# Ordering one more burst of state-space products, and moving the delta rule's output norm to GpSimd

## The chip, the cores and the metric

The kernel runs on one core of one Trainium2 chip. The metric is the device time of one execution in microseconds (us); less is better. TensorE does matmuls and transposes (PE in the profile, with its weight loads as PEld), VectorE is DVE, ScalarE is ACT, GpSimd is POOL, and SyncE (SP) issues the DMAs.

## The reference, cut to what matters

Two layers of a decoder trunk, 512 tokens, 1024 channels, float32. Each layer norms x, projects it into three branches (a chunked state-space scan, latent attention, a gated delta rule), merges them with sigmoid gates, and adds a squared-ReLU feed-forward. The change touches two branches. In the state-space scan, for each chunk of 128 tokens (a "block" below), the part within the block is

```python
L = jnp.exp(jnp.where(tril, A_cum[..., :, None] - A_cum[..., None, :], -jnp.inf))
CB = jnp.einsum('bclgn,bcsgn->bcgls', Cc, Bc)
y_diag = jnp.einsum('bcgls,bgecls,bcsgep->bclgep', CB, L, X)
```

and in the delta rule the recurrence's output o is normed per head and gated:

```python
o = gated_delta_chunked(q, k, v, g, beta)
o = rmsnorm(o, norm_g) * jax.nn.silu(z.astype(jnp.float32).reshape(Bsz, S, GDN_V_HEADS, GDN_HEAD_V))
```

## The kernel before, in words

Everything is float32. The large products (projections, output products, feed-forward) are made as three passes of a split operand: a weight tile of 128x512 is cast on ScalarE to its high part (`whi`, L170), VectorE subtracts to get the low part (`wlo`, L171), and TensorE adds high times high, high times low and low times high (`mm3`, L198 to L200). There are four buffers of each part. These products make up most of the program; below they are called the dense products. Their outputs sit in four PSUM banks (`acc`). Small products (state-space, delta rule, transposes) run in plain float32, into three further banks (`sm`, `sm_bank()`) and one called `yt`.

A framework orders the instructions of each engine when the program is built: by priority, which is mostly the order of the program text, among those that its own model of time finds ready. On the chip each engine then runs its list strictly in order. The small products come earlier in the text than the dense products of the stage after them, so the framework fits them among these. `place(key, ins)` notes a dense product under (tag, row k, column j), and `behind(key, ins)` forces a small product to stand after the noted one on TensorE's list; this is an order at build time and no wait on the chip.

`ssd_group(g, ...)` handles one half of the state-space branch (g is 0 or 1), for the four blocks t = 0 to 3. For each block it makes the decay tiles `e2` (two of four heads each; four buffers `eE`), multiplies them by the masked product `cb` of L782, and then makes the eight decay products of L791, each with 64 output columns, two heads side by side into halves of one bank, `py`. L802 is the carried state's part (`po`), L809 the new state (`pst`), L823 a sum of squares. The dense products that surround it are those of `out_proj` for the attention branch, tags (ly, 1, 2g, "g") and (ly, 1, 2g, "y"). The L791 products of blocks 0 and 3 are put behind named rows; those of blocks 1 and 2 are left to the framework.

`gdn_unit(u, ...)` handles four of the delta rule's eight heads, again over four blocks t. Its chain from block to block is: L1067 (state times keys), L1070 (DVE), L1073 (`pw`), L1078 and L1084 (`vn` on DVE, `vd` on ACT), L1087 (`pS`), L1096 (new state, DVE). Off that chain it makes the output: L1099 (`po`), L1106 (`pq`), ACT copies `po` to the tile `o` (L1107, or L1111 in block 0), DVE adds `pq` (L1109), ACT takes the squares' sums into `ss` (L1115). Then DVE makes the norm's factor `ms` from `ss` and the query's norm (L1119 to L1124, with a power -0.5 on GpSimd at L277), and scales: `gz = gz * ms * o`, one instruction per head (L1127). The tile `o` has one buffer (`wk3`), so L1107 of a block waits until L1127 of the block before has read it. After the four blocks, L1132 transposes `gz`. Around unit 0 run the dense products of unit 1's keys and values with their convolutions (L724 on ACT, L728 three times on DVE for each bank), around unit 1 those of `out_proj` for the delta branch.

Of the kernel before, what the change touches and what calls it, by code (L numbers as in the profile page):

```python
# [10 lines left out]
F32 = mybir.dt.float32  # L11
# [4 lines left out]
ALU = mybir.AluOpType  # L16
# [4 lines left out]
P = 128  # L21
S = 512
T = S // P
D = 1024
KD = D // P
EPS = 1e-6
# [29 lines left out]
def hybrid_kernel(ctx, tc, a, out, depth=2, taps=None):  # L56
    nc = tc.nc
    pe, act, dve, pool, sync = nc.tensor, nc.scalar, nc.vector, nc.gpsimd, nc.sync
    uid = itertools.count()

    def mk(pl, shape, dt, tag, bufs=None):
        return pl.tile(shape, dt, tag=tag, name=f"{tag}_{next(uid)}", bufs=bufs)
# [12 lines left out]
    def bc_last(ap, n):  # L75
        sh = list(ap.shape)
        return ap.unsqueeze(len(sh)).to_broadcast(sh + [n])

    cst = ctx.enter_context(tc.tile_pool(name="cst", bufs=1))
    sp = ctx.enter_context(tc.tile_pool(name="sp", bufs=1))  # L80
# [9 lines left out]
    def y_bank():  # L90
        return mk(ps_sm, [P, 512], F32, "yt", 1)

    def sm_bank():
        return mk(ps_sm, [P, 512], F32, "sm")
# [11 lines left out]
    nhalf = mk(cst, [P, 32], F32, "nhalf")  # L106
# [43 lines left out]
    def after_product(i, o):  # L150
        tc.add_manual_dep(i, o.name, order_only, reason="behind a product")

    def behind(key, ins):

        if key in seen_at:
            after_product(ins.ins, seen_at[key])
        else:
            awaiting.setdefault(key, []).append(ins.ins)
# [116 lines left out]
    def rsq(o, ss, scale, eps, exp=None):  # L275
        dve.tensor_scalar(o, ss, scale, eps, ALU.mult, ALU.add)
        pool.tensor_tensor(o, o, (exp if exp is not None else nhalf)[:, : o.shape[1]], ALU.pow)  # L277
# [106 lines left out]
    for ly in range(depth):  # L384
# [97 lines left out]
        def seg_exp(o, t, h0):  # L482

            of = o.rearrange("p i l -> p (i l)")
            sync.dma_start(of, d_c[t, h0 * P : (h0 + 4) * P].partition_broadcast(P))
            for i in range(4):
                act.activation(o[:, i], o[:, i], AF.Relu, scale=-1.0, bias=cum[:, t, h0 + i : h0 + i + 1])  # L487
            act.activation(of, of, AF.Exp, scale=-1.0)
# [99 lines left out]
        for hp in range(4):  # L588
# [68 lines left out]
            for j in range(2):  # L657
# [3 lines left out]
                for t in range(T):  # L661
                    n = max(256, (t + 1) * P)
                    tok = slice(t * P, (t + 1) * P)
                    ps = sm_bank()
                    o = ps[:, :n]
# [5 lines left out]
                    n = (t + 1) * P  # L671
                    o = ps[:, :n]
# [9 lines left out]
                for kbs in ((0,), (1,), (3, 2)):  # L682
                    ps = sm_bank()
                    n = 0
# [14 lines left out]
                    for kb, c0, c in parts:  # L699
                        v_h, v_l = (x[:, kb, :] for x in vs[j])  # L700
                        o = po[:, c0:]
# [34 lines left out]
        br = bp.enter_context(tc.tile_pool(name="br", bufs=1, reuse_waits="tile"))  # L736


        def ssd_group(g, yh, yl):
# [12 lines left out]
            for t in range(T):  # L752
                x = pe.transpose(ps[:, t * P : (t + 1) * P], bt[:, t * P : (t + 1) * P], ident)
# [19 lines left out]
            c4 = lambda x: x.rearrange("p (c l) -> p c l", c=4)  # L773
            pss = y_bank()
            st = None
            for t in range(T):
                tok = slice(t * P, (t + 1) * P)
                e2 = [mk(br, [P, 4, P], F32, "eE", 4) for _ in range(2)]
                for q in range(2):
                    seg_exp(e2[q], t, h0 + 4 * q)  # L780
                ps = sm_bank()
                pe.matmul(ps[:, :P], bt[:, tok], ctl[:, tok], start=True, stop=True)  # L782
                cb = mk(br, [P, P], F32, "gk", 2)
                dve.scalar_tensor_tensor(cb, ps[:, :P], 0.25, incl, ALU.mult, ALU.mult)
                for e in e2:
                    dve.tensor_tensor(e, e, bc_mid(cb, 4), ALU.mult)
                py = sm_bank()
                for c in range(4):
                    for i in range(2):
                        h = 2 * c + i  # L790
                        x = pe.matmul(py[64 * i : 64 * i + 64, c * P : (c + 1) * P], xd[:, t, h * 64 : (h + 1) * 64], e2[h // 4][:, h % 4, :], start=True, stop=True)  # L791
                        if t in (0, T - 1):
                            behind(((ly, 1, 2 * g, "g"), 2, 0) if t == 0 else ((ly, 1, 2 * g, "y"), 3, 0), x)
                y = xf[:, :, tok]
                dve.tensor_tensor(y, y, c4(py), ALU.add)
                if t > 0:
                    eb = mk(br, [P, 4, P], F32, f"wk{t % 2}")
                    for i in range(2):
                        sync.dma_start(eb[64 * i : 64 * i + 64], d_p.rearrange("t (n l) -> t n l", l=P)[t, h0 + i : h0 + 8 : 2].partition_broadcast(64))
                    po = sm_bank()  # L800
                    for c in range(4):
                        pe.matmul(po[:, c * P : (c + 1) * P], st[:, c * P : (c + 1) * P], ctl[:, tok], start=True, stop=True)  # L802
                    dve.tensor_tensor(eb, c4(po), eb, ALU.mult)
                    dve.tensor_tensor(y, y, eb, ALU.add)
                if t < T - 1:
                    xe = mk(br, [P, 512], F32, "wk3")
                    dve.tensor_tensor(hv8(xe), hv8(xd[:, t, :]), bc_last(dec[:, 1, t, h0 : h0 + 8], 64), ALU.mult)
                    pst = sm_bank()
                    pe.matmul(pst, btok[:, t, :], xe, start=True, stop=True)  # L809
                    sn = mk(br, [P, 512], F32, "st", 2)  # L810
                    if t == 0:
                        act.copy(sn, pst)
                    else:
                        dve.tensor_tensor(hv8(sn), hv8(st), bc_last(dec[:, 2, t, h0 : h0 + 8], 64), ALU.mult)
                        dve.tensor_tensor(sn, sn, pst, ALU.add)
                    st = sn
                zt = z[:, :, tok]
                dve.tensor_tensor(zt, zt, y, ALU.mult)
                sq = mk(br, [P, 4, P], F32, "wk2")
                act.activation(sq, zt, AF.Square)  # L820
                dve.tensor_tensor(sq[:, 0:2], sq[:, 0:2], sq[:, 2:4], ALU.add)
                dve.tensor_tensor(sq[:, 0], sq[:, 0], sq[:, 1], ALU.add)
                x = pe.matmul(pss[:, t : t + 1], sq[:, 0], ones[:, 0:1], start=True, stop=True)  # L823
                if t > 1:
                    behind(((ly, 1, 2 * g, "y"), 4 * t - 5, 0), x)
# [19 lines left out]
        hv = lambda x: x.rearrange("p (h n) -> p h n", h=4)  # L845
# [159 lines left out]
        def gdn_unit(u, kT, ork, cc, cd, Yt, yh, yl):  # L1005
# [10 lines left out]
            rq = mk(sp, [P, 2, T], F32, "grq", 2)  # L1016
# [8 lines left out]
            gz = mk(br, [P, T, 512], F32, "tok", 5)  # L1025
            for i in range(2):
                for j, pj in enumerate(dense_F(weights(w_in, O_GV + (4 * u + 2 * i) * P, 256, D), tiles(256), D, xh, xl, tag=(ly, "v", 4 * u + 2 * i))):
                    h = 2 * i + j
# [3 lines left out]
                    for t in range(T):  # L1032
                        x = pe.transpose(ps[:, t * P : (t + 1) * P], vf[:, t * P : (t + 1) * P], ident)
# [5 lines left out]

            hdec = lambda i, t, h: dec[:, i, t, hd0 + h : hd0 + h + 1]  # L1040
            ss = mk(sp, [P, T, 4], F32, "gos", 2)
            g_, y_ = ((ly, 2, i // 2, "gy"[i % 2]) for i in range(2))
            seq = [(ly, "k", 2), (ly, "v", 4), (ly, "v", 6)] if u == 0 else [g_, y_, (ly, 2, 1, "g")]
            pw_place = (seq[0], 3, 0), (seq[0], 7, 0), (seq[1], 2, 0)
# [4 lines left out]
            for t in range(T):  # L1049
# [5 lines left out]
                for i in range(2):  # L1055
                    x = pe.matmul(pg[:, i * P : (i + 1) * P], kT[i][:, tok], qT[i][:, tok], start=True, stop=True)
# [15 lines left out]
                for h in range(4):  # L1072
                    x = pe.matmul(pw[:, h * P : (h + 1) * P], Y[:, h, :], r[:, h * P : (h + 1) * P], start=True, stop=True)  # L1073
# [6 lines left out]
                if t < T - 1:  # L1080
# [5 lines left out]
                    for i in range(2):  # L1086
                        x = pe.matmul(pS[:, i * 256 : (i + 1) * 256], ktok[i][:, t, :], vd[:, i * 256 : (i + 1) * 256], start=True, stop=True)  # L1087
# [10 lines left out]
                for h in range(4):  # L1098
                    x = pe.matmul(po[:, h * P : (h + 1) * P], pt_[:, h, :], vn[:, h * P : (h + 1) * P], start=True, stop=True)  # L1099
                    if t == T - 1:  # L1100
                        behind((seq[1], 2, 1), x)
                o = mk(br, [P, 512], F32, "wk3")
                if t > 0:
                    pq = sm_bank()
                    for i in range(2):
# [8 lines left out]
                    jk = mk(br, [P, P], F32, "gk", 2)  # L1114
                    act.activation(jk, o[:, h * P : (h + 1) * P], AF.Square, accum_out=ss[:, t, h : h + 1])  # L1115

                rqt = mk(sp, [P, 4], F32, "grt", 2)
                for j in range(2):
                    dve.tensor_scalar(rqt.rearrange("p (i j) -> p i j", j=2)[:, :, j], rq[:, :, t], 128.0 ** -0.5, None, ALU.mult)  # L1119
                ms = mk(sp, [P, 4], F32, "gms", 2)  # L1120
                dve.tensor_tensor(ms, ss[:, t, :], rqt, ALU.mult)
                dve.tensor_tensor(ms, ms, rqt, ALU.mult)
                rsq(ms, ms, 1.0 / 128, EPS)
                dve.scalar_tensor_tensor(ms, ms, 0.5, rqt, ALU.mult, ALU.mult)  # L1124
                for h in range(4):
                    gzh = hv(gz[:, t, :])[:, h]
                    dve.scalar_tensor_tensor(gzh, gzh, ms[:, h : h + 1], hv(o)[:, h], ALU.mult, ALU.mult)  # L1127
            for c in range(4):
                k = 4 * u + c
                ps = y_bank()  # L1130
                for t in range(T):
                    x = pe.transpose(ps[:, t * P : (t + 1) * P], gz[:, t, c * P : (c + 1) * P], ident)  # L1132
# [132 lines left out]
        with tc.tile_pool(name="wo", bufs=1, reuse_waits="tile") as wo:  # L1265
# [8 lines left out]
            h = mk(hpl, [P, T, D], F32, "h")  # L1274
# [209 lines left out]
```

## Time and profile before

| what | value |
|---|---|
| median of 3 runs | 2274.53 us (2274.5 to 2274.64) |
| the profiled execution | 2274.29 us, of which the profile's span is 2272.5 us |
| PE busy | 2252.4 us, 99% of the span |
| DVE busy | 1649.5 us, 73% |
| ACT busy | 1186.1 us, 52% |
| POOL busy | 65.0 us, 3%, 84 instructions |
| granted TensorE clock | 0.999 |

A profile row of the timeline gives start, duration, engine, line, operation, the tiles written and read, and how many instructions were merged. A plain float32 matmul leaves two records. In a row of the waits, the numbers are total us, how often, and the longest. The shown end of a matmul is modelled, and matmuls overlap; the distance from start to start tells what one cost.

### The profile page before, as it was taken

The numbers are of one execution on the slowest core, as the hardware profiler recorded it, in microseconds if no ns is written. First come the engines' busy times: TensorE is split into PE (matmuls) and PEld (weight loads), VectorE is DVE, ScalarE is ACT, GpSimd is POOL, SyncE is SP. The second block draws the span as 40 slices with busy tenths as digits, with TensorE's granted clock in tenths as the row PEclk, the third lists the DMA queues.
The fourth block names the chain that finished last, engine by engine and source line by source line (L and its number), as shares of the span: only waits on it lengthen the run. The fifth ranks groups of instructions, "written<-read, shape, count | busy, mean of one in ns | idle before, by whom it ended". The sixth has DMA issues, their size and how long they took to land.

```text
span 2272.5 us, 32127 instructions
## 1 busy us (share of the span) xinstructions
PE 2252.4 (99%) x11758; PEld 1867.6 (82%) x11758; DVE 1649.5 (73%) x3315; ACT 1186.1 (52%) x2444; POOL 65.0 (3%) x84
## 2 busy tenths in 40 slices
PE   9999999999999999999999999999999999999998
PEld 8888888888888888888888878888888887888886
DVE  7886567776766778767868865678657667778668
ACT  6666744333443555554656667443344435645545
POOL 1000000000000000000010000000001000000000
PEclk9999999999999999999999999999999999999999
DMA  4223633442225143233132246335422251433231
GB/s 143 81 75 110 190 108 119 137 134 75 84 65 176 56 149 111 93 110 103 52 99 81 71 121 195 104 110 148 121 84 75 66 189 34 167 112 102 84 111 47
DMA packets 220030, 244.07 MB, mean 107 GB/s; under 512 B 34256, under 2 KB 172384, under 8 KB 219872
## 3 DMA queue, kind: packets, MB, share of 16 engines
q1 hardware_dynamic: 219872, 242.02, 34.7%
q8 instruction: 92, 1.51, 0.3%
q14 instruction: 66, 0.54, 0.1%
HBM read 225.53 MB, written 11.74 MB: 104 GB/s over the span
## 4 chain that ended last, share of the span: by engine, by line
PE 95%; DVE 3%; DMA 1%; ACT 1%; issue 0%; POOL 0%; SPq 0%; DVEq 0%; POOLq 0%; ACTq 0%
PE acc L198 24%; PE acc L200 24%; PE acc L199 24%; PE sm L200 3%; PE sm L199 3%; PE sm L198 3%; PE sm L687 1%; PE sm L791 1%; DVE wlo L171 1%; PE yt L703 1%; PE sm L1073 1%; PE sm L802 1%; PE sm L1099 1%; PE yt L200 1%; PE yt L199 1%; PE yt L198 1%
## 5 line engine op out<-in xcount | busy, mean ns | idle before, releaser
L171 DVE TENSOR_TENSOR wlo<-wraw,whi 128x512 fp32r<-128x512 f32 (+1 forms) x536 | 365.4, 686 | 336.3 <-ACT whi L170 325.3
L170 ACT CAST whi<-wraw 128x512 fp32r<-128x512 f32 (+1 forms) x536 | 329.5, 618 | 524.1 <-PE acc L199 339.7
L198 PE MATMUL acc<-xh,whi 128*128 128x512 f32 (+1 forms) x1344 | 525.3, 391 | 0.0
L200 PE MATMUL acc<-xh,wlo 128*128 128x512 f32 (+1 forms) x1344 | 520.4, 388 | 0.0
L199 PE MATMUL acc<-xl,whi 128*128 128x512 f32 (+1 forms) x1344 | 519.2, 387 | 0.0
L200 PEld LDWEIGHTS acc<-xh,wlo 128*128 128x128 f32 x1344 | 252.5, 188 | 49.3
L198 PEld LDWEIGHTS acc<-xh,whi 128*128 128x128 f32 x1344 | 252.5, 188 | 48.4 <-ACT xh L272 0.4
L199 PEld LDWEIGHTS acc<-xl,whi 128*128 128x128 f32 x1344 | 252.7, 188 | 47.6 <-DVE xl L273 0.7
L170 ACT CAST whi<-wr 128x512 fp32r<-128x512 f32 x168 | 104.3, 621 | 107.9 <-PE acc L199 47.7
L198 PE MATMUL acc<-yh,whi 128*128 128x512 f32 x384 | 152.1, 400 | 0.0
L199 PE MATMUL acc<-yl,whi 128*128 128x512 f32 x384 | 150.3, 391 | 0.0
L200 PE MATMUL acc<-yh,wlo 128*128 128x512 f32 x384 | 149.8, 390 | 0.0
L171 DVE TENSOR_TENSOR wlo<-wr,whi 128x512 fp32r<-128x512 f32 x168 | 113.1, 685 | 35.6 <-ACT whi L170 34.7
L728 DVE SCALAR_TENSOR_TENSOR ckl<-acc,pc,ckl 128x511 f32<-128x511 f32 (+2 forms) x168 | 121.2, 743 | 19.2 <-ACT ckl L724 10.9
L198 PEld LDWEIGHTS acc<-yh,whi 128*128 128x128 f32 x384 | 71.5, 188 | 16.4 <-ACT yh L272 2.2
L200 PEld LDWEIGHTS acc<-yh,wlo 128*128 128x128 f32 x384 | 72.1, 188 | 15.1
L199 PEld LDWEIGHTS acc<-yl,whi 128*128 128x128 f32 x384 | 72.1, 188 | 14.2
L198 PE MATMUL acc<-whi,xh 128*128 128x512 f32 (+1 forms) x208 | 80.3, 386 | 1.2 <-DVE ckl L728 1.2
L199 PE MATMUL acc<-wlo,xh 128*128 128x512 f32 (+1 forms) x208 | 79.3, 381 | 0.0
L200 PE MATMUL acc<-whi,xl 128*128 128x512 f32 (+1 forms) x208 | 79.2, 382 | 0.0
L1219 DVE TENSOR_TENSOR h<-h,acc 128x512 f32<-128x512 f32 x120 | 76.9, 679 | 1.3 <-PE acc L200 1.3
L487 ACT ACTIVATE eE<-eE,cum 128x128 f32<-128x128 f32 x192 | 62.5, 390 | 27.9 <-DMA eE<-d_c 26.2
(468 smaller groups left out, 4497.8 us busy)
## 6 DMA issues: line engine op xcount, KB each, us to landing
wraw<-in_w_in_dram SPq DMA_DIRECT2D x144, 512.0 KB, 3.6
wraw<-in_w_up_dram SPq DMA_DIRECT2D x64, 512.0 KB, 3.5
wr<-in_w_down_dram SPq DMA_DIRECT2D x32, 1024.0 KB, 5.1
eE<-d_c SPq DMA_DIRECT2D x48, 256.0 KB, 4.1
wraw<-in_w_mla_out_dram SPq DMA_DIRECT2D x16, 512.0 KB, 3.4
eE<-d_e SPq DMA_DIRECT2D x32, 256.0 KB, 2.9
wraw<-in_w_ssd_out_dram SPq DMA_DIRECT2D x16, 512.0 KB, 3.3
wraw<-in_w_gdn_out_dram SPq DMA_DIRECT2D x16, 512.0 KB, 3.5
```

The source lines that it names most:

```text
L170: act.copy(hi, raw)
L171: dve.tensor_tensor(lo, raw, f32(hi), ALU.subtract)
L198: pe.matmul(o, ah, bh, start=start, stop=False, skip_group_check=more)
L199: pe.matmul(o, ah, bl, start=False, stop=False, skip_group_check=more)
L200: return pe.matmul(o, al, bh, start=False, stop=stop, skip_group_check=more)
L487: act.activation(o[:, i], o[:, i], AF.Relu, scale=-1.0, bias=cum[:, t, h0 + i : h0 + i + 1])
L687: pe.transpose(ps[:, n : n + P], pn[t][:, kb * P : (kb + 1) * P], ident)
L703: pe.matmul(o, v_h, th[:, c : c + w], start=kb == 0, stop=False)
L728: dve.scalar_tensor_tensor(acc[:, d:], ps[:, : S - d], taps_[3 - d], acc[:, d:], ALU.mult, ALU.add)
L791: x = pe.matmul(py[64 * i : 64 * i + 64, c * P : (c + 1) * P], xd[:, t, h * 64 : (h + 1) * 64], e2[h // 4][:, h % 4, :], start=True, stop= ...
L802: pe.matmul(po[:, c * P : (c + 1) * P], st[:, c * P : (c + 1) * P], ctl[:, tok], start=True, stop=True)
L1219: dve.tensor_tensor(hs_, hs_, ps[t], op)
```

## The change

Three edits, all in the two functions above.

1. The L791 products of block 1 are put behind row 4, column 1 of (ly, 1, 2g, "g"). Blocks 0 and 3 keep their places.
2. The tile `o` of the delta rule alternates between the buffers `wk3` and `wk0` from block to block.
3. The norm's factor and the scaling go from VectorE to GpSimd. The query's factors for all four blocks are prepared once for each unit (`rq1`, `rq2`). For each block GpSimd first multiplies `gz` by `o` (128x512), then makes `ms` from `ss` in four small instructions (the power among them), then multiplies `gz` by `ms`, spread over each head's 128 columns (128x512). The ten VectorE instructions of a block go.

```diff
             st = None
+            burst_place = {0: ("g", 2, 0), 1: ("g", 4, 1), T - 1: ("y", 3, 0)}
             for t in range(T):
...
-                        if t in (0, T - 1):
-                            behind(((ly, 1, 2 * g, "g"), 2, 0) if t == 0 else ((ly, 1, 2 * g, "y"), 3, 0), x)
+                        if t in burst_place:
+                            behind(((ly, 1, 2 * g, burst_place[t][0]), *burst_place[t][1:]), x)
...
             ss = mk(sp, [P, T, 4], F32, "gos", 2)
+            rq1, rq2 = (mk(sp, [P, T, 4], F32, n, 2) for n in ("grt", "grs"))
+            for j in range(2):
+                pool.tensor_scalar(rq1.rearrange("p t (i j) -> p i t j", j=2)[:, :, :, j], rq, 128.0 ** -0.5, None, ALU.mult)
+            pool.tensor_tensor(rq2, rq1, rq1, ALU.mult)
+            pool.tensor_scalar(rq1, rq1, 0.5, None, ALU.mult)
...
-                o = mk(br, [P, 512], F32, "wk3")
+                o = mk(br, [P, 512], F32, f"wk{3 - 3 * (t % 2)}")
...
-                rqt = mk(sp, [P, 4], F32, "grt", 2)
-                for j in range(2):
-                    dve.tensor_scalar(rqt.rearrange("p (i j) -> p i j", j=2)[:, :, j], rq[:, :, t], 128.0 ** -0.5, None, ALU.mult)
+                pool.tensor_tensor(gz[:, t, :], gz[:, t, :], o, ALU.mult)
                 ms = mk(sp, [P, 4], F32, "gms", 2)
-                dve.tensor_tensor(ms, ss[:, t, :], rqt, ALU.mult)
-                dve.tensor_tensor(ms, ms, rqt, ALU.mult)
-                rsq(ms, ms, 1.0 / 128, EPS)
-                dve.scalar_tensor_tensor(ms, ms, 0.5, rqt, ALU.mult, ALU.mult)
-                for h in range(4):
-                    gzh = hv(gz[:, t, :])[:, h]
-                    dve.scalar_tensor_tensor(gzh, gzh, ms[:, h : h + 1], hv(o)[:, h], ALU.mult, ALU.mult)
+                pool.tensor_tensor(ms, ss[:, t, :], rq2[:, t, :], ALU.mult)
+                pool.tensor_scalar(ms, ms, 1.0 / 128, EPS, ALU.mult, ALU.add)
+                pool.tensor_tensor(ms, ms, nhalf[:, :4], ALU.pow)
+                pool.tensor_tensor(ms, ms, rq1[:, t, :], ALU.mult)
+                pool.tensor_tensor(hv(gz[:, t, :]), hv(gz[:, t, :]), bc_last(ms, P), ALU.mult)
```

## The prediction

> **What bounds the kernel now.** I read the page first: the span, the busy shares and the chain that ended last.
>
> ```profile
> span 2272.5 us, 32127 instructions
> PE 95%; DVE 3%; DMA 1%; ACT 1%; issue 0%; POOL 0%; SPq 0%; DVEq 0%; POOLq 0%; ACTq 0%
> ```
>
> TensorE carries 95% of the chain. So the change is worth what it takes out of TensorE's own sequence: extra time inside bursts of small products, and waits. Work taken from VectorE is worth nothing unless TensorE waited for it. Next I read the waits, in total per pair of lines, for the lines that the change touches.
>
> ```profile
> ACT wk L1107 <- DVE tok L1127: 14.0, 6, 3.6
> ...
> PE sm L1067 <- ACT wk L1107: 1.2, 2, 0.6
> PE acc L198 <- DVE ckl L728: 1.2, 2, 0.6
> ```
>
> ScalarE stood 14.0 us in six waits until VectorE's scaling had read the single output tile. TensorE itself waited in this stage only twice for that copy (once in each layer), and twice for a convolution tap on VectorE. These four places and the bursts of L791 are all that the change can win.
>
> **Part 1, the decay products of block 1.** The timeline of TensorE in the first group of the first layer, for block 1 and then for block 2, which nobody orders and which comes whole:
>
> ```profile
> 231.33 0.40 PE L198 MATMUL acc<-xh,whi 128*128 128x512 f32 x1
> 231.66 0.43 PE L791 MATMUL sm<-eE,tok 128*64 128x128 f32 x2
> 232.02 0.38 PE L823 MATMUL yt<-ct,wk 128*128 128x1 f32 x2
> 232.34 0.65 PE L791 MATMUL sm<-eE,tok 128*64 128x128 f32 x6
> 232.92 0.71 PE L802 MATMUL sm<-ckh,st 128*128 128x128 f32 x4
> 233.56 0.66 PE L791 MATMUL sm<-eE,tok 128*64 128x128 f32 x8
> 234.15 0.71 PE L802 MATMUL sm<-ckh,st 128*128 128x128 f32 x4
> ...
> 236.01 0.39 PE L200 MATMUL acc<-xh,wlo 128*128 128x512 f32 x1
> ...
> 238.77 0.39 PE L200 MATMUL acc<-xh,wlo 128*128 128x512 f32 x1
> 239.09 1.09 PE L791 MATMUL sm<-eE,tok 128*64 128x128 f32 x16
> 240.11 1.16 PE L802 MATMUL sm<-ckh,st 128*128 128x128 f32 x8
> ...
> 242.03 0.39 PE L198 MATMUL acc<-xh,whi 128*128 128x512 f32 x1
> ...
> 242.73 0.39 PE L198 MATMUL acc<-xh,whi 128*128 128x512 f32 x1
> ...
> 244.26 0.40 PE L200 MATMUL acc<-xh,wlo 128*128 128x512 f32 x1
> ```
>
> The step of a dense product is (242.73 - 242.03) / 3 = 0.23 us. Block 1's burst has 16 records of L791, 8 of L802, 2 of L823, 2 of L809, 2 of L782. From 231.33 to 236.01 are 4.68 us with two dense steps: 4.22 us for the burst. Block 2 does the same products in two stretches: 238.77 to 242.03 with four dense steps (L791, L802, L823), 3.26 - 0.92 = 2.34 us; 242.73 to 244.26 with two (L809, L782), 1.53 - 0.46 = 1.07 us; together 3.41 us. So the split of L791 in three costs 4.22 - 3.41 = 0.81 us. In it, the first two records take 0.36 us until L823 starts, where sixteen in a row take 1.02.
>
> The change holds all eight products until row 4, column 1. Then they are released at one moment and all decay tiles are there, so I expect one run of sixteen. What stands behind them: L802 of block 1 follows on TensorE's list, as its bank is taken after `py`; VectorE's additions to y wait for `py` and come later, by the six further dense steps in which the burst moves from row 4, column 0 to row 4, column 1 (some 8 products, 1.9 us). The cover for that is the framework's freedom: block 2 is not ordered, and dense products fill in until it is ready. The buffers `eE` of block 3 come free 1.9 us later too. Four bursts of this kind (two groups, two layers): 4 x 0.81 = 3.2 us less. Bounds: a gain of 3.6 (no second stretch either), and a loss of 3.2, if the same split then falls on block 2 and block 1 still splits. I take 3.2, by the burst next to it.
>
> **Part 2, the alternating tile and the stalls of TensorE.** The two places of the first layer, behind the busy time by stretch (us of length, then PE, PEld, DVE, ACT, POOL):
>
> ```profile
> 617.00:637.00 20.00, 19.42 (x103) 15.97 (x103) 16.52 (x41) 9.79 (x22) 2.91 (x3) 1.00 0.28 83
> ...
> 606.69 0.39 PE L200 MATMUL acc<-xh,wlo 128*128 128x512 f32 x1
> ...
> 607.04 0.58 ACT L1107 COPY wk<-sm 128x512 f32<-128x512 f32 x1 [2.28 <-DVE tok L1127]
> ...
> 607.68 1.13 PE L1067 MATMUL sm<-st,ft 128*128 128x256 f32 x4 [0.60 <-ACT wk L1107]
> ...
> 630.57 0.61 DVE L1127 SCALAR_TENSOR_TENSOR tok<-tok,gms,wk 128x128 f32<-128x128 f32 x2
> ...
> 631.70 0.23 DVE L1119 TENSOR_SCALAR grt<-grq 128x2 f32<-128x2 f32 x2
> ...
> 634.41 2.05 DVE L728 SCALAR_TENSOR_TENSOR ckl<-acc,pc,ckl 128x511 f32<-128x511 f32 x3
> ...
> 634.99 0.39 PE L200 MATMUL acc<-whi,xl 128*128 128x512 f32 x1
> ...
> 635.95 0.47 PE L198 MATMUL acc<-whi,xh 128*128 128x512 f32 x1 [0.58 <-DVE ckl L728]
> ```
>
> At 606.69 TensorE needs a bank that L1107 has not yet copied out, because L1107 waits for L1127 of the block before. Start to start is 0.99 us where a step is 0.23: a stall of 0.76. With two tiles the copy waits only for L1099, so the stall goes whole. At 634.99 TensorE waits for a tap of the convolution: 0.96 - 0.23 = 0.73 us. No idle time is noted before these VectorE rows, and 0.61 + 0.23 = 0.84 us of the work just ahead is scaling and factors of the delta rule, which leave; the rest of block 3's output also moves earlier, as its copy no longer waits. 0.84 is more than 0.73, so I let this stall go too. What is late next there is the next bank's tap, one conversion later, and nothing shows it. Two layers: 2 x (0.76 + 0.73) = 3.0 us less. Bounds: 0 to 3.0.
>
> **Part 3, the work on GpSimd.**
>
> ```profile
> L1127 DVE SCALAR_TENSOR_TENSOR tok<-tok,gms,wk x64: 339/345/353, 588.2 to 1821.4; 128x128 f32<-128x128 f32 x64
> ...
> L277 POOL TENSOR_TENSOR gms<-gms,nhalf 128x4 f32<-128x4 f32 x16 | 17.8, 1114 | 283.9 <-DVE gms L276 283.9
> L277 POOL TENSOR_TENSOR nrs<-nrs,nhalf 128x1 f32<-128x1 f32 x20 | 12.3, 626 | 902.1 <-DVE nrs L293 844.0 <-DVE nrs L276 58.1
> ...
> L519 POOL TENSOR_TENSOR yh<-yh,lrs 128x256 f32<-128x256 f32 x8 | 5.6, 728 | 0.2
> ```
>
> VectorE loses 64 x 0.345 = 22 us of scaling and the small ones beside it; off the path, but for the stall above. GpSimd gets, for each of 16 blocks, two 128x512 products and three small ones beside the power it already does. A 128x512 product: between 0.73 us (no more than 128x256) and twice that, 1.46; I take 1.46, since the elements double. A small one: the power costs (1.114 - 0.626) / 3 = 0.16 us per element, so 0.46 of it is fixed; between 0 and 1.1, I take 0.46. A block is then 2 x 1.46 + 3 x 0.46 + 1.11 = 5.4 us of GpSimd, 22 us for a unit, where unit 0 lasts from 588.2 (the first L1127) to 630.6 (its last, above); the few further ones at a unit's head are hidden the same way. From the last square to the finished tile: 3 x 0.46 + 1.11 + 1.46 = 3.95 us.
>
> ```profile
> 692.07 0.16 DVE L1121 TENSOR_TENSOR gms<-gos,grt 128x4 f32<-128x4 f32 x1 [0.20 <-ACT gk L1115]
> ...
> 697.10 0.60 PE L1132 MATMUL yt<-ct,tok 128*128 128x128 f32 x4
> ```
>
> In unit 1 the sums are there at 692.07, the tile at about 696.0, the transposes at 697.10: 1.1 us to spare. With small ones at 1.1 each it would be 697.9 and a stall of 0.8, twice: 1.6 us. I take 0.
>
> **What GpSimd does to VectorE.** The timeline of the one place where GpSimd multiplies beside VectorE now:
>
> ```profile
> 34.21 0.42 DVE L135 TENSOR_SCALAR qh<-qh 128x512 f32<-128x512 f32 x1
> ...
> 35.14 0.83 DVE L136 TENSOR_SCALAR qh<-qh 128x512 f32<-128x512 f32 x1
> ...
> 34.22 2.79 POOL L519 TENSOR_TENSOR yh<-yh,lrs 128x256 f32<-128x256 f32 x4
> ```
>
> Two VectorE instructions of one shape: 0.42 us for the one that started first, 0.83 beside GpSimd. So a 128x512 product on GpSimd can hold a VectorE instruction up, by up to its own 1.46 us, and what stands behind that on VectorE, the chain L1070, L1078, L1096 above all. The weight subtractions (L171) alone come once in twelve dense products, 0.69 us in 2.7. There are 32 such products; if half meet one and lose 0.7 us (half of 1.46), VectorE loses 11 us. TensorE waited at L1067 in two of the twelve blocks that have one, 1 in 6, and for convolution taps, many more in number, also twice; between the two I let one ninth of it through: 1.2 us. Bounds: 0 and 11.
>
> The Trainium skill says it more sharply (SBUF — State Buffer, "Who interferes with whom"): a VectorE instruction with two SBUF inputs and a GpSimd instruction that reads SBUF exclude each other, and the later one waits for the whole of the other. The rows above agree with a wait of that order, 0.41 us. By that rule VectorE's instructions with one input in PSUM (L1070, L1078, L1096) would not be held themselves, only by an L171 or L1062 ahead of them; the sum by it lies between the 1.2 and the 11 us.
>
> **The sum.** -3.2 - 3.0 + 1.2 = -5.0 us. The profiled execution, 2274.29 us (span 2272.5 and 1.8 around it), is within 0.3 us of the median, 2274.53, so the forecast is 2269.5 us, 0.22% faster.
>
> **The rivals.**
> - Contention decides (slower). Place: the delta rule's blocks, 32 products on GpSimd against VectorE's chain. If all 11 us reach TensorE: 2274.5 - 6.2 + 11 = 2279.3. It decides from 6.2 us on, that is 9 of 32 meetings at 0.7 us. For it: the 0.83 row, and VectorE is busy 16.5 of the 20 us from 617 on. Against it: the dense products wait for no low part there, and the chain's VectorE steps read PSUM.
> - Part 1 only moves the split to block 2, whose tiles are finished late because `py` of block 1 is. Then 0 instead of 3.2: 2272.7, no change. For it: block 2's products came 3 us after block 1's burst. Against: with nothing forced they came whole before.
> - The stalls of part 2 do not go, but the next wait (the next bank, the tap behind an L171 held by GpSimd) takes their place: 2274.5 - 3.2 + 1.2 = 2272.5, no change. For it: the same 16.5 of 20 us.
>
> **How the numbers follow.** My forecast 0.50, contention 0.13, the split moved 0.22, the stalls staying 0.15. The measurement tells 0.2%, 4.5 us, from no change, and the forecast is just beyond it: of its 0.50 I count 0.48 as faster, together with 0.03 where part 1 or 2 fails and a further wait goes instead; the rest of the three is same, 0.35; slower, with contention in full or a longer tail, 0.14. The forecast's own range is 2267 to 2272. The range that holds 8 of 10 reaches from 2266.0 (3.6 + 3.0 and no contention is 2267.9, and 2 us for further small waits on VectorE that go) to 2276.5 (contention at two thirds of 11 us, with both gains).
>
> **What would show it.** Step 1: L791 as x16 at all blocks, and about 0.8 us less around block 1. Step 2: no wait of L1107 for a scaling, none of L1067 for L1107, no stall near 635. Step 3: GpSimd busy some 70 us more, L1132 of unit 1 not waiting. Contention: longer L171 and L1062, and new waits of TensorE for L1070, L1078 or L1084. The prediction is wrong if block 2 splits, or if TensorE's steps in the four units grow by over 6 us.

## The result, and the profile after

| | before | after |
|---|---|---|
| median | 2274.64 us (13 runs, 2273.3 to 2275.93) | 2278.97 us (13 runs, 2277.18 to 2280.96) |
| profiled execution | 2274.29 us, span 2272.5 | 2278.69 us, span 2276.9 |
| DVE busy | 1649.5 us | 1631.5 us |
| POOL busy | 65.0 us | 121.7 us |

The ratio after to before is 1.002, with a 95% interval from 1.0011 to 1.0028. The change costs 4.3 us where 5.0 us less were forecast, and 2278.97 lies above the forecast range. Lines of the changed kernel are 1 to 6 higher than before (L791 is now L792, L823 L824, L829 L830, L1062 L1068, L1070 L1076, L1073 L1079).

The page after, the chain that ended last by engine:

```profile
PE 94%; DVE 2%; DMA 1%; ACT 1%; issue 1%; POOL 0%; SPq 0%; DVEq 0%; POOLq 0%; ACTq 0%
```

TensorE still bounds the kernel, so the 4.3 us must be found in its sequence again. Its waits after (total us, times, longest); of the new pairs, these three stand in stages that the change edits (a fourth, 0.5 us for L272 at L198, stands 11 us from the start):

```profile
PE sm L1079 <- DVE tok L1076: 1.9, 4, 0.5
...
PE sm L1105 <- DVE eE L1068: 0.9, 2, 0.5
...
PE sm L830 <- POOL srs L277: 0.3, 1, 0.3
```

Both rows of TensorE that the change was to remove (L1067 for L1107, L198 for L728) are gone. A wait for VectorE (L1079 for L1076) has come four times, in the delta rule too. The timeline of the changed kernel there, first unit, block 1:

```profile
596.01 1.29 POOL L1123 TENSOR_TENSOR tok<-tok,wk 128x512 f32<-128x512 f32 x1 [6.73 <-DVE wk L1115]
596.07 1.78 DVE L171 TENSOR_TENSOR wlo<-wraw,whi 128x512 fp32r<-128x512 f32 x1 [0.20 <-ACT whi L170]
...
596.28 0.58 PE L198 MATMUL acc<-xh,whi 128*128 128x512 f32 x1
...
598.10 1.11 DVE L1076 SCALAR_TENSOR_TENSOR tok<-sm,ndec,tok 128x128 f32<-128x128 f32 x4
...
598.49 1.26 PE L1079 MATMUL sm<-tok,tok 128*128 128x128 f32 x8 [0.47 <-DVE tok L1076]
...
599.51 0.47 PE L198 MATMUL acc<-xh,whi 128*128 128x512 f32 x1
```

The same place in the timeline of the kernel before:

```profile
594.05 0.69 DVE L171 TENSOR_TENSOR wlo<-wraw,whi 128x512 fp32r<-128x512 f32 x1 [0.20 <-ACT whi L170]
...
594.26 0.58 PE L198 MATMUL acc<-xh,whi 128*128 128x512 f32 x1
...
594.99 1.11 DVE L1070 SCALAR_TENSOR_TENSOR tok<-sm,ndec,tok 128x128 f32<-128x128 f32 x4
...
596.65 0.48 PE L198 MATMUL acc<-xh,whi 128*128 128x512 f32 x1
```

The new GpSimd product begins 0.06 us ahead of a weight subtraction (L171). That takes 1.78 us where it took 0.69, L1076 begins later by as much, and TensorE waits for it. TensorE runs the same dense products in the same order in both traces, so their starts can be set side by side. Here the two L198 around the wait stand 3.23 us apart (596.28 to 599.51) where they stood 2.39 apart (594.26 to 596.65): 0.84 us lost. At block 1 of the four units it is 0.84, 0.85, 0.85 and 0.83: 3.4 us. All VectorE time of L171, by group, before and then after:

```profile
L171 DVE TENSOR_TENSOR wlo<-wraw,whi 128x512 fp32r<-128x512 f32 (+1 forms) x536 | 365.4, 686 | 336.3 <-ACT whi L170 325.3
```

```profile
L171 DVE TENSOR_TENSOR wlo<-wraw,whi 128x512 fp32r<-128x512 f32 (+1 forms) x536 | 372.7, 700 | 353.7 <-ACT whi L170 340.4
```

The subtractions cost 7.3 us more, 4 x 1.09 = 4.4 of it at these four places. The rest falls elsewhere in the units; in unit 1 of both layers, which has one more of 1.78 us, TensorE loses no more than at block 1.

More is lost in the state-space block. TensorE's timeline after, first group, blocks 1 and 2 and the norm's sum of block 2 (L824):

```profile
232.32 0.39 PE L199 MATMUL acc<-xl,whi 128*128 128x512 f32 x1
232.55 0.32 PE L824 MATMUL yt<-ct,wk 128*128 128x1 f32 x2
...
233.04 0.40 PE L198 MATMUL acc<-xh,whi 128*128 128x512 f32 x1
...
234.20 0.39 PE L200 MATMUL acc<-xh,wlo 128*128 128x512 f32 x1
234.52 1.09 PE L792 MATMUL sm<-eE,tok 128*64 128x128 f32 x16
...
237.54 0.48 PE L198 MATMUL acc<-xh,whi 128*128 128x512 f32 x1
...
241.74 0.39 PE L198 MATMUL acc<-yh,whi 128*128 128x512 f32 x1
242.05 0.43 PE L792 MATMUL sm<-eE,tok 128*64 128x128 f32 x2
242.42 0.38 PE L824 MATMUL yt<-ct,wk 128*128 128x1 f32 x2
242.73 0.65 PE L792 MATMUL sm<-eE,tok 128*64 128x128 f32 x6
...
243.73 0.66 PE L792 MATMUL sm<-eE,tok 128*64 128x128 f32 x8
...
246.09 0.48 PE L199 MATMUL acc<-yl,whi 128*128 128x512 f32 x1
...
249.17 0.39 PE L200 MATMUL acc<-yh,wlo 128*128 128x512 f32 x1
249.49 1.09 PE L792 MATMUL sm<-eE,tok 128*64 128x128 f32 x16
...
251.43 0.48 PE L198 MATMUL acc<-yh,whi 128*128 128x512 f32 x1
251.75 0.35 PE L824 MATMUL yt<-ct,wk 128*128 128x1 f32 x2
...
252.28 0.39 PE L200 MATMUL acc<-yh,wlo 128*128 128x512 f32 x1
```

The sum of block 2 before, directly ahead of the burst of block 3:

```profile
248.39 0.39 PE L200 MATMUL acc<-yh,wlo 128*128 128x512 f32 x1
248.62 0.28 PE L823 MATMUL yt<-ct,wk 128*128 128x1 f32 x2
248.82 1.09 PE L791 MATMUL sm<-eE,tok 128*64 128x128 f32 x16
```

Block 1 comes whole: from 234.20 to 237.54 with one dense step is 3.34 - 0.23 = 3.11, and its sum, now among dense products, adds 0.72 - 0.46 = 0.26 (232.32 to 233.04). That is 3.37 where it was 4.22: 0.85 less. But block 2 now comes in three parts, as block 1 did: 241.74 to 246.09 is 4.35 - 0.23 = 4.12 where it was 3.41, 0.71 more. And the norm's sum of block 2, which stood directly ahead of block 3's burst before, now stands alone: 251.43 to 252.28 is 0.85 for two steps, 0.39 too long. Ahead of the burst it had cost 0.11 (248.39 to 248.82 is 0.43; without the sum, 249.17 to 249.49, it is 0.32).

Set side by side over the whole program, the changed kernel loses 2.3 us in the four state-space groups and 1.4 us in the four units of the delta rule (3.4 at block 1, less what the removed stalls gave back). The remaining 0.7 lies in stages without an edit.

### The profile page after: what moved, and what is told of

Read it like the earlier page. It is cut to its first block, busy times and chain, and to the rows that moved or that the text cites. A ratio compares the mean times of both kernels' runs of the same rounds, so it can differ in the third digit from the quotient of the medians.

```text
span 2276.9 us, 32088 instructions
## 1 busy us (share of the span) xinstructions
PE 2255.7 (99%) x11758; PEld 1867.7 (82%) x11758; DVE 1631.5 (72%) x3155; ACT 1184.6 (52%) x2444; POOL 121.7 (5%) x180
## 4 chain that ended last, share of the span: by engine, by line
PE 94%; DVE 2%; DMA 1%; ACT 1%; issue 1%; POOL 0%; SPq 0%; DVEq 0%; POOLq 0%; ACTq 0%
PE acc L198 24%; PE acc L200 24%; PE acc L199 24%; PE sm L199 3%; PE sm L200 3%; PE sm L198 3%; PE sm L687 1%; PE sm L792 1%; DVE wlo L171 1%; PE sm L1105 1%; PE yt L703 1%; PE sm L1079 1%; PE sm L308 1%; PE sm L803 1%; PE yt L199 1%
## 5 line engine op out<-in xcount | busy, mean ns | idle before, releaser
L171 DVE TENSOR_TENSOR wlo<-wraw,whi 128x512 fp32r<-128x512 f32 (+1 forms) x536 | 372.7, 700 | 353.7 <-ACT whi L170 340.4
L198 PE MATMUL acc<-xh,whi 128*128 128x512 f32 (+1 forms) x1344 | 525.1, 391 | 0.0
L200 PE MATMUL acc<-xh,wlo 128*128 128x512 f32 (+1 forms) x1344 | 519.9, 387 | 0.0
L200 PEld LDWEIGHTS acc<-xh,wlo 128*128 128x128 f32 x1344 | 252.5, 188 | 49.6
L198 PEld LDWEIGHTS acc<-xh,whi 128*128 128x128 f32 x1344 | 252.5, 188 | 48.4 <-ACT xh L272 0.4
L198 PE MATMUL acc<-yh,whi 128*128 128x512 f32 x384 | 152.2, 400 | 0.0
L200 PE MATMUL acc<-yh,wlo 128*128 128x512 f32 x384 | 149.8, 390 | 0.0
L728 DVE SCALAR_TENSOR_TENSOR ckl<-acc,pc,ckl 128x511 f32<-128x511 f32 (+2 forms) x168 | 120.8, 743 | 26.5 <-ACT ckl L724 18.1
L171 DVE TENSOR_TENSOR wlo<-wr,whi 128x512 fp32r<-128x512 f32 x168 | 113.2, 686 | 34.9 <-ACT whi L170 34.0
L198 PEld LDWEIGHTS acc<-yh,whi 128*128 128x128 f32 x384 | 71.5, 188 | 16.9 <-ACT yh L272 2.3
L200 PEld LDWEIGHTS acc<-yh,wlo 128*128 128x128 f32 x384 | 72.1, 188 | 14.8
L198 PE MATMUL acc<-whi,xh 128*128 128x512 f32 (+1 forms) x208 | 80.1, 385 | 0.0
L200 PE MATMUL acc<-whi,xl 128*128 128x512 f32 (+1 forms) x208 | 79.2, 382 | 0.0
L198 PE MATMUL acc<-whi,yh 128*128 128x512 f32 x192 | 75.0, 390 | 1.2 <-DVE h L1221 1.2
```

Source lines behind the costliest of these rows:

```text
L171: dve.tensor_tensor(lo, raw, f32(hi), ALU.subtract)
L198: pe.matmul(o, ah, bh, start=start, stop=False, skip_group_check=more)
L200: return pe.matmul(o, al, bh, start=False, stop=stop, skip_group_check=more)
L728: dve.scalar_tensor_tensor(acc[:, d:], ps[:, : S - d], taps_[3 - d], acc[:, d:], ALU.mult, ALU.add)
```

## The experiments

Every kernel is compared with the kernel before on the same chip, whose median was 2274.1 to 2274.3 us. An interval of a ratio is some 2 us wide to either side. "Theory" and "rival" are the two outcomes that were named before each run.

**The two halves apart.** Edit 1 alone:

```diff
+            burst_place = {0: ("g", 2, 0), 1: ("g", 4, 1), T - 1: ("y", 3, 0)}
...
-                        if t in (0, T - 1):
-                            behind(((ly, 1, 2 * g, "g"), 2, 0) if t == 0 else ((ly, 1, 2 * g, "y"), 3, 0), x)
+                        if t in burst_place:
+                            behind(((ly, 1, 2 * g, burst_place[t][0]), *burst_place[t][1:]), x)
```

> The kernel before with the order of block 1's decay products alone. Theory (from the trace after: block 1 whole gains 0.88 us in a group, block 2 now split costs 0.74, block 3 and the sum behind it 0.3 to 0.6): 0.2 to 0.5 us slower in each of four groups, 0.8 to 2 us slower in all. Rival (the prediction's step 1): 3.2 us faster.

Measured 2276.93 us, ratio 1.0013 (1.0004 to 1.0022): 2.8 us slower, somewhat more than the theory's 0.8 to 2. So the half that was to give 3.2 costs time by itself. Its trace shows what the changed kernel's shows: block 2 in three parts, the lone sum, and 0.3 us at L830. Set side by side with before at the same dense products, the first group is 0.8 us ahead behind block 1, level behind block 2 and 0.4 behind after the norm; the four groups lose 2.5 us.

Edits 2 and 3 alone (the diff of the change without `burst_place`; lines from L792 on are then one lower than in the changed kernel, so L1104 and L1067 here are L1105 and L1068 there):

> The kernel before with the alternating tile and GpSimd's work, the order of the decay products as before. Theory: block 1 of each unit loses 0.9 us to a weight subtraction held up by GpSimd's first product (4 x 0.9 = 3.6), the two stalls of TensorE in unit 0 go (3.0), some 0.7 of other waits come in unit 0: 1 to 2 us slower. Rival (the prediction's steps 2 and 3): 1.8 us faster.

Measured 2277.73 us, ratio 1.0016 (1.0008 to 1.0025): 3.6 us slower, more than the 1 to 2 expected. TensorE loses 0.83 us at block 1 of each unit, 3.3 in all. Side by side with before, the four units lose 1.4 us together, as in the changed kernel; the rest of this trace's loss lies outside what the edits touch (the table below).

**The alternating tile alone:**

```diff
-                o = mk(br, [P, 512], F32, "wk3")
+                o = mk(br, [P, 512], F32, f"wk{3 - 3 * (t % 2)}")
```

> The kernel before with the alternating output tile alone; VectorE keeps the factor and the scaling. Theory: the stall of TensorE behind the copy of the output goes in both layers (1.5 us), the one behind the convolution's tap stays or halves (0 to 1.5): 1.5 to 3 us faster. Rival (the stalls move to the next wait): no change.

Measured 2271.91 us, ratio 0.999 (0.9981 to 0.9999): 2.2 us faster. The stall at 606.7 goes; at 635 the step of 0.96 us shrinks to 0.54, so 0.31 of a stall of 0.73 is left. Unit 0 is 1.3 us shorter in each layer. TensorE also issues some of the delta rule's small products a few dense products earlier, so a part of the gain may be the order.

**Is it the first GpSimd product?** Edits 2 and 3, with that product back on VectorE:

```diff
-                pool.tensor_tensor(gz[:, t, :], gz[:, t, :], o, ALU.mult)
+                dve.tensor_tensor(gz[:, t, :], gz[:, t, :], o, ALU.mult)
```

> The delta rule's two edits, but with the first product of each block (gate times output, 128x512) on VectorE and the rest on GpSimd. Theory (GpSimd's first product holds the weight subtraction up): the 0.9 us of block 1 go in all four units, 1.5 to 3.5 us less than with both products on GpSimd. Rival (the new waits come from the changed order, not from GpSimd): as with both on GpSimd.

Measured 2273.95 us, ratio 0.9998 (0.9989 to 1.0007): 3.8 us below the same kernel with the product on GpSimd, a little over the 1.5 to 3.5 expected. Nothing is held up at block 1: no wait for L1075 and no subtraction over 0.9 us is left. A wait remains that edits 2 and 3 share with the change, 0.8 us of TensorE at L1104 for L1067.

The suspected cost alone, in the kernel before: one GpSimd product per unit whose result nobody reads.

```diff
+                if t == 1:
+                    dm = mk(br, [P, 512], F32, "wk0")
+                    pool.tensor_tensor(dm, gz[:, t, :], o, ALU.mult)
```

> The kernel before with one product more in block 1 of each unit: GpSimd multiplies the gate tile by the output into a free buffer (128x512), which nobody reads; nothing is left out. The order on TensorE, VectorE and ScalarE is the same as before. Theory (GpSimd's product holds up the weight subtraction that starts just behind it, and the state's chain behind that): 0.8 us more in each of four units, 3.3 us slower, with a weight subtraction of about 1.8 us. Rival (it was the changed order): no change.

Measured 2278.51 us, ratio 1.0019 (1.001 to 1.0027): 4.25 us slower, by four instructions. The orders of TensorE, VectorE and ScalarE are those of before. Its timeline:

```profile
594.75 1.28 POOL L1119 TENSOR_TENSOR wk<-tok,wk 128x512 f32<-128x512 f32 x1 [6.52 <-DVE wk L1109]
594.82 1.76 DVE L171 TENSOR_TENSOR wlo<-wraw,whi 128x512 fp32r<-128x512 f32 x1 [0.20 <-ACT whi L170]
...
597.23 1.26 PE L1073 MATMUL sm<-tok,tok 128*128 128x128 f32 x8 [0.45 <-DVE tok L1070]
```

The loss per place is 0.82, 0.87, 0.83 and 0.87 us up to the next dense product, and 3.7 us in the four units. So contention alone, with nothing else changed, costs this time.

**Is it the moment, or GpSimd's load (e12)?** Edits 2 and 3, with the same two products in the other order, so that both begin behind the power:

```diff
-                pool.tensor_tensor(gz[:, t, :], gz[:, t, :], o, ALU.mult)
...
                 pool.tensor_tensor(hv(gz[:, t, :]), hv(gz[:, t, :]), bc_last(ms, P), ALU.mult)
+                pool.tensor_tensor(gz[:, t, :], gz[:, t, :], o, ALU.mult)
```

> As e2_delta_only, but GpSimd multiplies the gate by the norm's factor first (as soon as the power is done) and by the output after that: the same instructions on GpSimd and the same work, the two products begin some 2.6 us later in each block. Theory A (the loss of 0.8 to 0.9 us in block 1 of each unit is the meeting of one GpSimd product with one L171, 594.66 against 594.72 in e2): L171 there is back at 0.69 us, no wait of L1078 for L1075 of 0.5, and the time is 3 us below e2_delta_only, about 2274.5; less if the later products meet L1067's tile (598) or another L171, which the rows would show as 1.2 to 1.8 us. Theory B (GpSimd's load as such slows VectorE, wherever it lies): the same time as e2, 2277 to 2278.

Measured 2273.44 us, ratio 0.9998 (0.9989 to 1.0006): 4.3 us below edits 2 and 3 in their own order, with the same work on GpSimd. Its timeline at the place:

```profile
594.24 0.69 DVE L171 TENSOR_TENSOR wlo<-wraw,whi 128x512 fp32r<-128x512 f32 x1 [0.20 <-ACT whi L170]
...
597.10 1.04 POOL L1127 TENSOR_TENSOR tok<-tok,gms 128x512 f32<-128x512 f32 x1
597.62 0.68 DVE L1083 TENSOR_TENSOR wk<-sm,gcc 128x512 f32<-128x512 f32 x1
598.22 0.74 DVE L728 SCALAR_TENSOR_TENSOR ckl<-acc,pc,ckl 128x510 f32<-128x510 f32 x1
598.22 1.30 POOL L1128 TENSOR_TENSOR tok<-tok,wk 128x512 f32<-128x512 f32 x1
598.94 1.13 DVE L171 TENSOR_TENSOR wlo<-wraw,whi 128x512 fp32r<-128x512 f32 x1
```

The first subtraction is back at 0.69. The products now meet L1083 and L728, which read a PSUM bank and keep their 0.68 and 0.74, and another L171, which is held to 1.13; TensorE does not wait for that one. The four units are 3.2 us shorter than before, where those of edits 2 and 3 are 1.4 longer. So it is the moment, not the load.

**The factor on GpSimd, the scaling on VectorE.** Edits 2 and 3, with both products back on VectorE as one scaling per head:

```diff
-                pool.tensor_tensor(gz[:, t, :], gz[:, t, :], o, ALU.mult)
...
-                pool.tensor_tensor(hv(gz[:, t, :]), hv(gz[:, t, :]), bc_last(ms, P), ALU.mult)
+                for h in range(4):
+                    gzh = hv(gz[:, t, :])[:, h]
+                    dve.scalar_tensor_tensor(gzh, gzh, ms[:, h : h + 1], hv(o)[:, h], ALU.mult, ALU.mult)
```

> The delta rule's two edits, but both 128x512 steps stay on VectorE as four scalings of 128x128; only the factor of 128x4 is made on GpSimd. Theory (it is the large products that hold VectorE up): no weight subtraction over 1 us in these units, and a time near that of the alternating tile alone, 1.5 to 3 us faster than before. Rival (any work on GpSimd's list behind the output costs the chain): 1 us slower or more.

Measured 2282.89 us (5 runs), ratio 1.0039 (1.0025 to 1.0053): 8.6 us slower: the theory is refuted, and the time falls on the rival's side (1 us slower or more), by much more than was expected. The rival's reason, that any work on GpSimd costs the chain, does not fit the run before (e12), which has more of it. The waits of VectorE, here and then before, and that of TensorE which follows here:

```profile
DVE tok L1129 <- POOL gms L1126: 22.9, 14, 3.2
```

```profile
DVE gms L1124 <- POOL gms L277: 14.0, 16, 1.1
```

```profile
PE yt L1134 <- DVE tok L1129: 3.4, 2, 1.7
```

VectorE's instructions stand in one line. It stood at most 1.1 us for GpSimd's power before; here it stands up to 3.2 us for the whole chain of four small instructions, with everything behind it. Moving both the factor and the scaling, as the change does, avoids that: no wait of VectorE for this factor is in its trace.

**All four bursts given a place (e7).** Edit 1, with block 2 named too, block 3 moved from row 3, column 0 to row 4, column 1, and L830 one row later:

```diff
-            burst_place = {0: ("g", 2, 0), 1: ("g", 4, 1), T - 1: ("y", 3, 0)}
+            burst_place = {0: ("g", 2, 0), 1: ("g", 4, 1), 2: ("y", 0, 1), T - 1: ("y", 4, 1)}
...
-            behind(((ly, 1, 2 * g + 1, "g"), 1, 0), pe.transpose(ps[:T, :P], rs, ident))
+            behind(((ly, 1, 2 * g + 1, "g"), 2, 0), pe.transpose(ps[:T, :P], rs, ident))
```

> The kernel before with the decay products of all four blocks put behind named rows (block 2 behind row 0, column 1 of the next product, block 3 behind row 4, column 1), and the norm's transpose one row later. On TensorE's list all four bursts are whole. Theory (the split goes to whatever block is left to the framework or comes due while the block before still has VectorE): 0.8 us less in each of four groups, 3.2 us faster. Rival (the bursts wait for their tiles, as VectorE's work moved too): no change or slower.

Measured 2276.21 us, ratio 1.0009 (1.0 to 1.0018): a miss. All bursts are whole, and each group is 0.6 to 1.0 us ahead by block 3, but behind it 0.6 us is lost in two of the groups and 1.6 to 1.7 in the other two. In the latter TensorE waits for the last sum, here by the waits:

```profile
PE yt L824 <- DVE wk L823: 1.6, 2, 0.9
```

With the alternating tile added (e9):

> All four bursts ordered and the output tile alternating, all of the norm on VectorE. Theory (the two gains lie in different stages and add): 3.2 + 2.2 = 5.4 us faster than before. Rival: no more than the alternating tile alone, 2.2 us faster.

Measured 2273.77 us, ratio 0.9999 (0.999 to 1.0008): 2.4 us below the one without it, the tile's worth again, but level with before where 5.4 or at least 2.2 less was expected.

The last sum and the transpose behind it let in later (e10), without the tile:

```diff
-                    behind(((ly, 1, 2 * g, "y"), 4 * t - 5, 0), x)
+                    behind(((ly, 1, 2 * g, "y"), 3, 0) if t == 2 else ((ly, 1, 2 * g + 1, "g"), 3, 0), x)
...
-            behind(((ly, 1, 2 * g + 1, "g"), 2, 0), pe.transpose(ps[:T, :P], rs, ident))
+            behind(((ly, 1, 2 * g + 1, "g"), 6, 0), pe.transpose(ps[:T, :P], rs, ident))
```

> As e7_all_bursts, but the sum of the norm of block 3 (L824) is let in about two rows of dense products later (some 6 products, 1.4 us) and the transpose of the factor (L830) behind it some 9 products after that. No wait of TensorE for L823 (e7: 0.9 us idle before L824) and none for L277's power before L830. Theory A (the decay products lie well when all four bursts are whole, and only the tail of block 3 gave the gain back): four groups by about 0.8 us, so -3 us, 2271.3; at least -2. Theory B (shorter bursts in a chain bound by VectorE's L822/L823 and the eviction only move the wait: the next wait appears wherever the next product that needs the tail stands, at L804/L839 or the following block): not below 2275, that is within 1 us of e7.

Measured 2273.78 us, ratio 0.9999 (0.999 to 1.0007): 2.4 us below the kernel without this edit and 2.5 above the 2271.3 of theory A, so between the two theories. The last sum no longer waits; in two groups the sum of block 2 does, and it stands alone:

```profile
249.33 0.39 PE L199 MATMUL acc<-yl,whi 128*128 128x512 f32 x1
250.35 0.35 PE L824 MATMUL yt<-ct,wk 128*128 128x1 f32 x2 [0.64 <-ACT eE L488]
250.56 0.48 PE L200 MATMUL acc<-yh,wlo 128*128 128x512 f32 x1
```

With the alternating tile added to that (e11):

> e10_later_sum together with the alternating output tile of the delta rule, nothing on GpSimd. Theory A: the two gains add, -3 and -2.2: about 2269.3, faster than the kernel before and the changed one; at least 1.5 us below e10. Theory B: only the tile's gain is left, 2272 to 2273. Between e9 and e3 the tile was worth 2.2 to 2.4 us, and that is expected again beside e10 by either.

Measured 2270.21 us, ratio 0.9982 (0.9973 to 0.9991): 4.0 us faster than before.

Last, with that tile, the sums of blocks 1 and 2 directly ahead of the next burst:

```diff
-                if t > 1:
-                    behind(((ly, 1, 2 * g, "y"), 3, 0) if t == 2 else ((ly, 1, 2 * g + 1, "g"), 3, 0), x)
+                if t > 0:
+                    behind((None, ((ly, 1, 2 * g, "y"), 0, 1), ((ly, 1, 2 * g, "y"), 4, 1), ((ly, 1, 2 * g + 1, "g"), 3, 0))[t], x)
```

> As e11_later_sum_alternate, but the norm's sums of blocks 1 and 2 (L824, two single-column products) stand directly ahead of the decay products of blocks 2 and 3 in place of among the dense products. Theory A (what the sums cost TensorE is their own place: in e11 a lone sum makes three dense steps 0.91 us long where they take 0.68, and two of the sums of block 2 wait 0.57 us on top): the waits go, 1.1 us for two groups, and eight sums lose 0.1 to 0.2 each beside a burst: 2 to 2.7 us below e11, about 2268. Theory B (a sum costs the same wherever it stands, and the later sum makes the next VectorE work late): the same time as e11 or up to 1 us more, 2270 to 2271.

Measured 2268.77 us, ratio 0.9976 (0.9967 to 0.9985): 5.4 us faster than before, the best of all. Against the kernel without this edit it is 1.4 us by the medians, within what separates two of them here. In the traces, the four groups together are 2.4 us shorter than without the edit, inside the 2 to 2.7 expected, and 3.5 us shorter than before; no row of a wait for L824 is left in its trace. Its timeline, block 3 of the first group:

```profile
250.77 0.28 PE L824 MATMUL yt<-ct,wk 128*128 128x1 f32 x2
250.98 1.09 PE L792 MATMUL sm<-eE,tok 128*64 128x128 f32 x16
```

And TensorE's time in the decay products by group, before, in the changed kernel and then in this one:

```profile
L791 PE MATMUL sm<-eE,tok 128*64 128x128 f32 x256 | 20.1, 281 | 0.0
```

```profile
L792 PE MATMUL sm<-eE,tok 128*64 128x128 f32 x256 | 20.5, 282 | 0.0
```

```profile
L792 PE MATMUL sm<-eE,tok 128*64 128x128 f32 x256 | 17.5, 279 | 0.0
```

With all bursts whole the same 256 records take 3.0 us less than in the changed kernel, which never had that gain. They take 17.5 us in all four kernels with whole bursts before this one too (e7, e9, e10, e11), so what those lacked was lost elsewhere; the edits that won it back move only the sums and the transpose.

**Where each kernel's time lies.** In these kernels TensorE runs the same 8688 dense products in the same order, so each profiled execution can be set beside that of the kernel before, stage by stage. Each figure is what the stage takes more (us, both layers):

| kernel | state-space groups | delta rule's units | elsewhere |
|---|---|---|---|
| the change | +2.3 | +1.4 | +0.7 |
| edit 1 (e1) | +2.5 | +0.1 | -0.2 |
| edits 2 and 3 (e2) | +1.1 | +1.4 | +2.9 |
| the tile alone (e3) | +0.3 | -2.7 | +0.6 |
| the factor first (e12) | +0.6 | -3.2 | +1.8 |
| all bursts (e7) | +1.4 | 0.0 | +0.4 |
| with the later sum and the tile (e11) | -1.1 | -2.7 | +0.2 |
| with the sums beside bursts (e13) | -3.5 | -2.6 | +0.1 |

Where a kernel edits nothing, its trace still differs: e2 by 1.1 us in the groups and by 2.9 elsewhere. Of the latter, 1.6 is one wait for a weight part (L200 for L171, 824 us from the start), and e2's profiled execution is 2.0 us above its median. How much of this the other executions share is not known.

## Why the prediction was wrong

The sum was -3.2 - 3.0 + 1.2 = -5.0; each term has a run of its own.

- **Part 1, the split: the step that failed.** "I expect one run of sixteen" held for block 1 (0.85 less in the first group, 0.81 said). The cover did not hold: "block 2 is not ordered, and dense products fill in until it is ready". That freedom is what broke block 2. This was the second rival, with the stated condition met ("the prediction is wrong if block 2 splits"), but its price of 0 was too kind: 0.85 - 0.71 leaves 0.14, and the sums that the old order had beside a burst came to stand alone. Edit 1 measured +2.8 for -3.2, a miss of 6.0. The size was about right: with all bursts whole and the sums beside them, the four groups are 3.5 us shorter. What makes the framework interleave block 2 was not tested; that naming its place ends it was.
- **Part 2, the stalls: right.** L1107's wait for the scaling and both stalls of TensorE are gone. The tile alone gives 2.2 where 3.0 were taken, 2.7 us in the units by its trace; 0.31 of the second stall stays in each layer there. It goes whole where the scaling has left VectorE too, as the prediction had it: with the factor first the units are 3.2 us shorter.
- **Contention: the mechanism was right, the share was wrong.** VectorE lost 7.3 us in L171 (11 at half of all meetings was the estimate). The step "I let one ninth of it through" failed: about half, 3.4 us at block 1 of the units, reached TensorE. I spread the meetings at random over 32 products, and they are not random. The order repeats in each unit, so if the product meets L171 in front of L1076 once, it does so four times. The extra product alone (4.25) and the two kernels that differ in this product's engine alone (3.8) agree; the term is +3.4 to +4.3 and not +1.2. The contention rival's place was right, its 11 us too many.
- **GpSimd's own time** was 1.29 and 1.04 us for the two products (1.46 taken) and 0.48, 0.19 and 0.32 for the small ones (0.46 taken), 57 us more in all where some 70 were said. The tail of unit 1 did not wait, as said. The rows of the two products:

```profile
L1123 POOL TENSOR_TENSOR tok<-tok,wk 128x512 f32<-128x512 f32 x16 | 20.6, 1287 | 228.8 <-ACT wk L1117 160.6 <-DVE wk L1115 46.4 <-ACT ft L1012 21.8
...
L1129 POOL TENSOR_TENSOR tok<-tok,gms 128x512 f32<-128x512 f32 x16 | 16.6, 1040 | 1.3
```

- **What was not foreseen:** TensorE waits 0.9 us at L1105 for L1068, in the first unit of both layers. It is there too when the first product is on VectorE (0.8), and gone when the factor goes first. Its cause was not tested.
- **A slip in the range:** two thirds of 11 us with both gains is 2274.5 - 6.2 + 7.3 = 2275.6, not 2276.5. The median lies above either.

The misses, 6.0 for the split, 0.8 for the stalls and 2.6 for the contention, add to 9.4 of the 9.5 us between forecast and median. This is closer than the runs allow: the halves alone, +2.8 and +3.6, sum to 6.4 where both together gave 4.3, and each median is uncertain by about 2 us. By the table the halves do add in the stages that they edit: 2.5 for the groups and 1.4 for the units alone, 2.3 and 1.4 together. What is over lies, in the trace of edits 2 and 3, where they change nothing.

The rule of the Trainium skill (SBUF — State Buffer, "Who interferes with whom") that VectorE with two SBUF inputs and a GpSimd instruction that reads SBUF exclude each other agrees with these traces. In the three meetings shown, the subtraction ends 0.55 us behind the end of the product (597.85 and 597.30; 596.58 and 596.03; 600.07 and 599.52), whenever it began. If it waited for the whole product it would end its own 0.69 behind; the 0.14 between is not explained here. L1083 and L728, with one input in PSUM, are not held, as the rule has it. The row that the prediction set beside the rule, L136, has one input. The kernel before had a meeting of the right kind 1.3 us later, where L138 otherwise takes 0.68:

```profile
36.43 1.13 DVE L138 SCALAR_TENSOR_TENSOR qh<-qh,qh 128x512 f32<-128x512 f32 x1
```

It ends at 37.56, again 0.55 behind the end of the GpSimd products that the prediction shows (34.22 and 2.79 long, to 37.01).

## What to carry to other kernels

An ordering that makes one burst whole must name the places of its neighbours too, and of the small products that stood beside it: here the ordering gave nothing until all four bursts, the sums and the transpose had places. Contention is priced by place, not by average: list what VectorE runs in the microsecond in which the new GpSimd product will start, and if a chain that TensorE waits for stands behind it, move the product, which took 4.3 us away here. VectorE time set free off the path is worth little: no version with the work on GpSimd had a median below that of the alternating tile alone, and in the units the best of them gained 0.5 us over the tile.

## What the runs showed of the hardware that I had not expected

A single 1.28 us product on GpSimd costs TensorE 0.82 to 0.87 us where a chain stands behind the VectorE instruction that it holds. And the same 128x512 product on GpSimd took 1.04 us with the second operand spread from 128x4, and 1.29 with two full operands.
